# Row order, gate placement and the FFN boundary of a two-layer diffusion backbone kernel, changed together

## The chip, the cores and the metric

The kernel runs on one core of one Trainium2 chip. The metric is the device time of one execution in microseconds (us), lower is better. All times below come from runs of the kernel before or from one profiled execution of it. Engine names are those of the profile: PE is the matrix engine, PEld its weight loads, DVE the vector engine, ACT the scalar engine, POOL and SP two further engines that here mostly issue transfers.

## The reference, cut to what matters

Two token streams of 256 tokens each, latent `x` and context `ctx`, of width 1024, pass two layers. A layer is a half-step SwiGLU FFN, a token mixer, and a second half-step FFN; each has its own adaLN shift, scale and gate, which come from `silu(c)` and `silu(c_ctx)` times a 1024 x 9216 matrix `w_ada` per layer.

```
mod = (silu(c) @ w_ada[l] + b_ada[l]).reshape(9, 1024)
u = rmsnorm(h, g) * (1 + scale) + shift
h = h + 0.5 * gate * ((silu(u @ w1) * (u @ w3)) @ w2)          # w1, w3: 1024 x 2816
z = u @ w_in                                                   # q, kv, pool, linear attention, gates
m = sum_i sigmoid(gates_i) * (branch_i @ w_branch[i])          # attention, pooling, linear attention
h = h + gate * (m @ w_out)
```

The context stream takes part up to the mixer of the last layer, where it gives keys, values and the start states of the linear attention; the second FFN of the last layer works on the 256 latent tokens alone. Inputs, weights and the output are fp32.

## The kernel before, in words

**Products.** Activations lie feature-major: a tile has 128 features on its partitions and 512 tokens along it, latent tokens in columns 0 to 255, context tokens in 256 to 511. Every fp32 operand is split into a rounded part (`whi`, `uhi`, `hi`) and a remainder (`wlo`, `ulo`, `lo`), and a product is three matmuls (`mm3`, L238, L239, L240). The rounded part of a weight tile is made on ACT (L190) and the remainder on DVE (L202), from a tile `raw` that SP loads. `Weights.run_ahead` does this ahead of the products: at most four `raw` tiles are loaded, and parts are cut while no more than `room` of the tiles are held (`ROOM_FFN`, `ROOM_MIX`, 20 each; `ROOM_1`, `ROOM_2` in the first FFN). All these tiles come out of one pool of 70 slots.

**Order.** The program is written as generators that are advanced by credits. Every engine then runs its instructions in the order in which they were placed, and waits at each for what it needs. In the mixers the chain of attention and linear attention yields names of steps, and `FILL` gives for each step how many pieces of other work (`fill`: the columns of `w_in` for pools, linear attention and gates, then the branch projections) are put behind it. `GATES` is the number of gate pieces among those put in while the pooling branch is made. When no such work is left before the attention's outputs `oa` are complete, the filler yields without work.

**Modulation (`ada`).** The 36 pieces (layer, j) of 512 columns of `w_ada` are made in the order of need. The first four of layer 0 are loaded by SP and multiplied on PE (L370, then four transposes, L384), j in the order 0, 2, 1, 3. Nearly all others are multiplied on DVE (`adaacc`, L401 and L403; 16 per piece, on tiles that POOL's queue loads), behind other work. Two pieces, (0, 17) and (1, 17), stand in `EDGE`: their products are on PE, at the start of the second FFN of layer 0 and of layer 1.

**Start.** `setup` transposes the normalised rows `xr` of `x` and `ctx` (32 transposes, L324), makes `csil` by Silu on ACT, and transposes the raw rows into the residual `h` in two parts. The first FFN's first units of weights are split into halves of four k tiles each.

**FFN start.** `ffn` takes the mean square of the residual by a matmul (`ms`, L508), `rstd` on ACT, and then u tile by tile: `ut` on DVE (L517), `uhi` on ACT, `ulo` on DVE (L521). The last FFN ends in token-major form: `ht`, 16 transposes of the residual (L715), and the gate `gt` by a matmul with a diagonal `dg` (L728) stand behind the first four of its 22 up units.

Of the kernel before, what the change touches and what calls it, by code (L numbers as in the profile page):

```python
# [38 lines left out]
NHALF, NSLOT, ROOM_FFN, ROOM_MIX, RAWS = 4, 70, 20, 20, 4  # L39
RAWS_ADA = 3  # L40
ROOM_1, ROOM_2, LAST = 16, 36, 4
# [4 lines left out]
GATES = (2, 12)  # L46
EDGE = {(1, 17): (1, 2), (0, 17): (0, 2)}
# [93 lines left out]

class Net:
    def __init__(self, nc, a, cst, msk, vecs, wa2, out, pools, w, wada):
# [6 lines left out]
        self.ahead = self.seconds = None  # L150
# [83 lines left out]
    def mm3(self, out, wts, x, start, stop):  # L234

        (wh, wl), (xh, xl) = wts, x
        mm = self.nc.tensor.matmul
        mm(out, wh, xh, start=start, stop=False)  # L238
        mm(out, wh, xl, start=False, stop=False)  # L239
        mm(out, wl, xh, start=False, stop=stop)  # L240
# [12 lines left out]
    def setup(self):  # L253
# [39 lines left out]
        self.act(out=self.csil[:, :, 0:2], in_=self.vec[0][:, V_C:V_C + 16].rearrange("p (s k) -> p k s", s=2), func=AF.Silu)  # L293
# [5 lines left out]
        for j in range(4):  # L299
# [5 lines left out]
            self.act(out=f, in_=f, func=AF.Exp, scale=-0.5)  # L305
# [5 lines left out]
        self.residual(range(4), [normed])  # L311
        self.hr = []
        for k in range(KD):
            t = self.slot(name="hr")
            if k % 2:
                self.act(out=t, in_=self.turned(xr, k), func=AF.Copy)
            else:
                nc.vector.tensor_copy(t, self.turned(xr, k))
            self.hr.append(t)

    def turned(self, x, k):
        ps = self.ps()
        for j in range(4):
            self.nc.tensor.transpose(ps[:, j * P:(j + 1) * P], x[j][k // 4][:, (k % 4) * P:(k % 4 + 1) * P], self.ident)  # L324
        return ps

    def residual(self, ks, others=()):
        for k in ks:
            if k < 4:
                i = self.nc.vector.tensor_copy(self.h[:, k, :], self.turned(self.xin, k))  # L330
                if self.tc:
                    self.behind(i, others)
            else:
                self.act(out=self.h[:, k, :], in_=self.turned(self.xin, k), func=AF.Copy)
# [24 lines left out]
    def ada(self, l, j):  # L359
# [4 lines left out]
        if early or self.on_pe:  # L364
            ps = self.ps("ada")
            for u in range(4):
                for k in range(2 * u, 2 * u + 2):
                    unit = None if early else self.ada_unit(l, j, k)
                    g = k % 4
                    nc.tensor.matmul(ps[32 * g:32 * g + 32, :], self.csil[:, k, :], self.early[j][k] if early else unit.hi,  # L370
                                     start=(k < 4), stop=(k >= 4))
# [8 lines left out]
            if not early or j in (1, 3):  # L380
                yield
# [7 lines left out]
            if early:  # L389
                yield  # L390
                if j in (0, 2):
                    yield
# [106 lines left out]
    def norm(self, l, i, n):  # L499
# [11 lines left out]
        def some(s, c, ks):  # L511
            for k in ks:
                assert {(l, i, k // 4), (l, i + 1, k // 4)} <= self.have
                if u[k] is None:
                    u[k] = self.slot(F32R, "uhi"), self.slot(F32R, "ulo")
# [30 lines left out]
    def first_norm(self):  # L546
# [3 lines left out]
        for ks in ([0], [1], [2, 3], range(4, KD)):  # L550
            for k in ks:
# [3 lines left out]
                for s in range(2):  # L555
                    c = slice(s * NL, (s + 1) * NL)
                    t, a, b = self.half("ut"), self.am[0][1][:, k, s:s + 1], self.mod[0][:, k, s:s + 1]
                    self.act(out=hi[:, c], in_=self.hr[k][:, c], func=AF.Identity, scale=a, bias=b)
# [49 lines left out]
    def ffn(self, l, which, n, final):  # L608
# [10 lines left out]
        if begin:  # L619
            norm = self.first_norm()  # L620
            self.adas(5)
            self.residual(range(4, KD))
            self.xin = None
            self.adas(5)
# [14 lines left out]
            first[1].extend(part(1, [0]))  # L639

            def rest():
# [3 lines left out]
                first[1].extend(part(1, [1, 2]))  # L645

        else:
            self.w.room = ROOM_FFN
            first = unit(0) + unit(1)
# [12 lines left out]
        def up(m0, m1):  # L662
            for m in range(m0, m1):
                if m == 0:
                    if begin:
                        steps = [lambda: None, lambda: self.adas(4), lambda: self.adas(1), lambda: self.adas(4), rest]
# [40 lines left out]
        up(0, 4)  # L707
        assert {(l, 8, 0), (l, 8, 1)} <= self.have

        ht = []  # L710
        for j in range(2):
            for c in range(2):
                ps = self.ps()
                for k in range(4):
                    nc.tensor.transpose(ps[:, k * P:(k + 1) * P], self.h[:, 4 * c + k, j * P:(j + 1) * P], self.ident)  # L715
# [798 lines left out]
```

## Time and profile before

The median of three runs is 2119.14 us (2117.68 to 2120.08). The profiled execution took 2120.19 us; the profile spans 2118.4 us of it, so 1.8 us lie around the span.

| | value |
|---|---|
| PE busy | 2071.1 us (98% of the span) |
| DVE busy | 1449.1 us (68%) |
| ACT busy | 883.3 us (42%) |
| DMA | 290.48 MB, mean 137 GB/s |
| matmuls of `ps<-uhi,whi` and its two partners | 3 x 1584 |
| DVE `wlo` / ACT `whi` | 912 each |
| DVE `adaacc` L403 | 420, mean 746 ns |

Starts of matmuls that follow one another without a wait are closer together than the busy time of one (the engine overlaps them), so how long a group of products takes is read from the distance of starts. "Idle before" names what ended an idle stretch. The granted clock (PEclk) is the share of full speed that the matrix engine was given in a stretch.

By places: the first FFN of layer 0 runs to about 404 us (the mean squares `ms` that begin the stages mark the places), its mixer to 866, its second FFN to 1243, the first FFN of layer 1 to 1609, its mixer to 1906, and the last FFN to the end.

### The profile page before, as it was taken

Reading aid. Unit: us, or ns where it says so; the run is one execution under the profiler, and the core shown is the slowest. Engines: PE = TensorE matmul, PEld = TensorE weight load, DVE = VectorE, ACT = ScalarE, POOL = GpSimd, SP = SyncE. Lnnn points to the kernel's source line nnn. Section 1 sums busy time; section 2 is a strip of 40 time slices with the busy share of each in tenths; the row PEclk is TensorE's granted clock in tenths of the full one; section 3 lists DMA queues with packets and bytes.
Section 4 is the critical chain, followed back from the end, with each engine's and each line's share of the span. In section 5 each row is a group of like instructions: output and inputs, shape, how many; then the busy total and the mean of one; then the engine's idle time right before and its main releaser. Section 6 shows DMA issues by size and latency. Waiting matters only on the chain.

```text
span 2118.4 us, 30235 instructions
## 1 busy us (share of the span) xinstructions
PE 2071.1 (98%) x11308; PEld 1738.7 (82%) x11308; DVE 1449.1 (68%) x2876; ACT 883.3 (42%) x1805; POOL 138.4 (7%) x264
## 2 busy tenths in 40 slices
PE   7999999999999999999999999999999999998999
PEld 4888888977777888788888898888888887897997
DVE  4789588875877664766965886685554688665564
ACT  5423223464445553432322343322343566654452
POOL 0011011000100000101110100010000000000000
PEclk9999999999999999999999999999999999999999
DMA  9557456424423223445744645473451343565663
GB/s 319 150 157 206 125 170 169 118 59 122 137 75 83 67 70 95 130 139 139 216 132 131 173 125 154 110 224 114 121 151 36 102 119 85 140 169 145 182 205 121
DMA packets 416836, 290.48 MB, mean 137 GB/s; under 512 B 18608, under 2 KB 388912, under 8 KB 416688
## 3 DMA queue, kind: packets, MB, share of 16 engines
q1 hardware_dynamic: 395920, 221.22, 37.0%
q0 software_dynamic: 20480, 67.13, 11.1%
q8 instruction: 89, 1.46, 0.3%
q14 instruction: 59, 0.48, 0.1%
q10 hardware_dynamic: 288, 0.20, 0.0%
HBM read 287.44 MB, written 1.05 MB: 136 GB/s over the span
## 4 chain that ended last, share of the span: by engine, by line
PE 52%; issue 41%; DMA 3%; DVE 2%; POOL 1%; ACT 0%; SPq 0%; POOLq 0%; DVEq 0%; ACTq 0%
PE ps L238 14%; PE ps L240 14%; PE ps L239 14%; DMA raw<-in_w_ada_dram 2%; PE fill L238 2%; PE fill L240 2%; PE fill L239 2%; DMA ada<-in_w_ada_dram 1%; POOL raw L355 1%; PE sc L1145 1%; DVE adaacc L403 1%; PE ada L370 1%; PE pt L1163 0%; PE av L1181 0%; DVE wlo L202 0%
## 5 line engine op out<-in xcount | busy, mean ns | idle before, releaser
L202 DVE TENSOR_TENSOR wlo<-raw,whi 128x512 fp32r<-128x512 f32 (+4 forms) x912 | 532.5, 618 | 103.3 <-ACT whi L190 92.0
L238 PE MATMUL ps<-uhi,whi 128*128 128x512 f32 (+1 forms) x1584 | 555.4, 353 | 7.8 <-ACT uhi L190 7.8
L239 PE MATMUL ps<-ulo,whi 128*128 128x512 f32 (+1 forms) x1584 | 554.8, 351 | 0.2 <-DVE ulo L560 0.2
L240 PE MATMUL ps<-uhi,wlo 128*128 128x512 f32 (+1 forms) x1584 | 554.5, 351 | 0.0
L190 ACT ACTIVATE whi<-raw 128x512 fp32r<-128x512 f32 (+4 forms) x912 | 467.7, 567 | 173.6 <-DMA raw<-in_ffn_w_dram 53.7
L238 PEld LDWEIGHTS ps<-uhi,whi 128*128 128x128 f32 x1584 | 299.6, 190 | 54.1 <-ACT uhi L190 12.0
L240 PEld LDWEIGHTS ps<-uhi,wlo 128*128 128x128 f32 x1584 | 300.7, 190 | 46.1 <-issue 5.8
L239 PEld LDWEIGHTS ps<-ulo,whi 128*128 128x128 f32 x1584 | 300.9, 190 | 40.6 <-issue 1.9
L403 DVE SCALAR_TENSOR_TENSOR adaacc<-raw,csil,adaacc 128x512 f32<-128x512 f32 x420 | 303.9, 746 | 32.7 <-DMA raw<-in_w_ada_dram 32.1
L238 PE MATMUL ps<-hi,whi 128*128 128x512 f32 (+1 forms) x738 | 271.2, 368 | 1.5 <-ACT hi L190 1.5
L240 PE MATMUL ps<-hi,wlo 128*128 128x512 f32 (+1 forms) x738 | 269.9, 366 | 0.0
L239 PE MATMUL ps<-lo,whi 128*128 128x512 f32 (+1 forms) x738 | 269.6, 366 | 0.0
L190 ACT ACTIVATE silu<-ps 128x512 f32<-128x512 f32 (+1 forms) x88 | 47.8, 543 | 495.7 <-PE ps L240 495.7
L355 POOL DMA_DIRECT2D raw<-in_w_ada_dram x256 | 137.4, 537 | 1783.2 <-DVE adaacc L401 713.7
L659 DVE TENSOR_TENSOR silu<-silu,ps 128x512 f32<-128x512 f32 (+1 forms) x88 | 54.5, 619 | 245.7 <-PE ps L240 140.0
L238 PE MATMUL fill<-uhi,whi 128*128 128x512 f32 (+1 forms) x576 | 204.2, 355 | 3.9 <-ACT whi L190 3.9
L240 PE MATMUL fill<-uhi,wlo 128*128 128x512 f32 (+1 forms) x576 | 196.7, 342 | 0.2 <-DVE wlo L202 0.2
L239 PE MATMUL fill<-ulo,whi 128*128 128x512 f32 (+1 forms) x576 | 196.2, 341 | 0.0
L238 PEld LDWEIGHTS ps<-hi,whi 128*128 128x128 f32 x738 | 139.1, 189 | 24.0 <-ACT hi L190 1.7
L239 PEld LDWEIGHTS ps<-lo,whi 128*128 128x128 f32 x738 | 139.2, 189 | 22.6 <-DVE lo L202 0.2
L240 PEld LDWEIGHTS ps<-hi,wlo 128*128 128x128 f32 x738 | 139.2, 189 | 22.6
L238 PEld LDWEIGHTS fill<-uhi,whi 128*128 128x128 f32 x576 | 110.0, 191 | 26.2 <-issue 8.5
(279 smaller groups left out, 2304.8 us busy)
## 6 DMA issues: line engine op xcount, KB each, us to landing
raw<-in_ffn_w_dram SPq DMA_DIRECT2D x192, 512.0 KB, 4.7
raw<-in_w_ada_dram POOLq DMA_DIRECT2D x256, 256.0 KB, 3.4
raw<-in_w_in_dram SPq DMA_DIRECT2D x86, 512.0 KB, 4.5
raw<-in_ffn_w_dram SPq DMA_DIRECT2D x48, 384.0 KB, 4.4
raw<-in_ffn_w_dram SPq DMA_DIRECT2D x48, 320.0 KB, 3.8
raw<-in_w_branch_dram SPq DMA_DIRECT2D x48, 256.0 KB, 2.9
ada<-in_w_ada_dram SPq DMA_DIRECT2D x32, 256.0 KB, 5.4
raw<-in_w_out_dram SPq DMA_DIRECT2D x16, 512.0 KB, 5.0
```

Of the source, the lines that this page charges most:

```text
L190: i = self.nc.scalar.activation(**k)
L202: second = lambda: self.nc.vector.tensor_tensor(out=lo, in0=src, in1=f32hi, op=ALU.subtract)
L238: mm(out, wh, xh, start=start, stop=False)
L239: mm(out, wh, xl, start=False, stop=False)
L240: mm(out, wl, xh, start=False, stop=stop)
L355: self.nc.gpsimd.dma_start(out=t, in_=src)
L370: nc.tensor.matmul(ps[32 * g:32 * g + 32, :], self.csil[:, k, :], self.early[j][k] if early else unit.hi, start=(k < 4), stop=(k >= 4))
L403: nc.vector.scalar_tensor_tensor(out=acc[s], in0=unit.hi, scalar=c, in1=acc[s], op0=ALU.mult, op1=ALU.add)
L659: nc.vector.tensor_tensor(out=s[:, 0:n], in0=s[:, 0:n], in1=p3[:, 0:n], op=ALU.mult)
L1145: nc.tensor.matmul(sc[:, 0:nk], q[h][:, tt * P:(tt + 1) * P], keys[h][:, k0:T], start=True, stop=True)
```

## The change

**Constants.** `ROOM_MIX` becomes 20 for the first mixer and 28 for the second; `ROOM_1` goes from 16 to 12; `GATES` from (2, 12) to (4, 12); a new `LATER` (0, 16); `EDGE` is empty, so (0, 17) and (1, 17) are made on DVE as all the others.

**Start.** `csil` is made from Exp, an add, a reciprocal and a multiplication. Of the raw rows' 32 transposes 24 come first, then the products of j 0, then the transposes of `xr`, then the last 8. The first product of j 1 and of j 3 is placed behind the last weight product before it. The second halves of all three first units are cut one step earlier (`more`).

**Second mixer.** u lies in a tile for each stream (`ul`, `uc`: rounded part and remainder of the 256 tokens side by side), and the context's tiles are let go once the linear attention's columns are made. The columns for its keys are made as 2 x 256 instead of 512 tokens. While the attention's outputs are incomplete, gates 0 to 7 and 16 to 23 are put in rather than nothing.

**Last FFN.** `ht` is made before the mean square (`by_tokens`), and `gt` behind eight up units.

```diff
...
-NHALF, NSLOT, ROOM_FFN, ROOM_MIX, RAWS = 4, 70, 20, 20, 4
+NHALF, NSLOT, ROOM_FFN, ROOM_MIX, RAWS = 4, 70, 20, (20, 28), 4
 RAWS_ADA = 3
-ROOM_1, ROOM_2, LAST = 16, 36, 4
+ROOM_1, ROOM_2, LAST = 12, 36, 4
...
-GATES = (2, 12)
-EDGE = {(1, 17): (1, 2), (0, 17): (0, 2)}
+GATES = (4, 12)
+LATER = (0, 16)
+EDGE = {}
...
+class Streams:
+
+
+    def __init__(self, lat, ctx):
+        self.lat, self.ctx = lat, ctx
+
+    def __getitem__(self, at):
+        c = at[1]
+        assert c.stop <= NL or c.start >= NL
+        return self.lat[:, c] if c.stop <= NL else self.ctx[:, c.start - NL:c.stop - NL]
...
-        self.act(out=self.csil[:, :, 0:2], in_=self.vec[0][:, V_C:V_C + 16].rearrange("p (s k) -> p k s", s=2), func=AF.Silu)
+        c, e = self.vec[0][:, V_C:V_C + 16], self.tiny(16, "esil")
+        self.act(out=e, in_=c, func=AF.Exp, scale=-1.0)
+        nc.vector.tensor_scalar(out=e, in0=e, scalar1=1.0, scalar2=None, op0=ALU.add)
+        nc.vector.reciprocal(out=e, in_=e)
+        by_k = lambda t: t.rearrange("p (s k) -> p k s", s=2)
+        nc.vector.tensor_tensor(out=self.csil[:, :, 0:2], in0=by_k(c), in1=by_k(e), op=ALU.mult)
...
         self.xin = xin
-        self.residual(range(4), [normed])
+        self.residual(range(6), (normed, last))
+        self.adas(4)
         self.hr = []
         for k in range(KD):
             t = self.slot(name="hr")
             if k % 2:
-                self.act(out=t, in_=self.turned(xr, k), func=AF.Copy)
+                self.act(out=t, in_=self.turned(xr, k, self.products), func=AF.Copy)
             else:
-                nc.vector.tensor_copy(t, self.turned(xr, k))
+                nc.vector.tensor_copy(t, self.turned(xr, k, self.products))
             self.hr.append(t)
-
-    def turned(self, x, k):
+        self.residual(range(6, KD))
+        self.xin = None
+        self.adas(1)
...
+    def residual(self, ks, others=None):
         for k in ks:
-            if k < 4:
-                i = self.nc.vector.tensor_copy(self.h[:, k, :], self.turned(self.xin, k))
-                if self.tc:
-                    self.behind(i, others)
+            ps = self.turned(self.xin, k)
+            if k % 2:
+                i = self.act(out=self.h[:, k, :], in_=ps, func=AF.Copy)
             else:
-                self.act(out=self.h[:, k, :], in_=self.turned(self.xin, k), func=AF.Copy)
+                i = self.nc.vector.tensor_copy(self.h[:, k, :], ps)
+            if self.tc and others:
+                self.behind(i, [others[k % 2]])
...
+                    g = k % 4
                     unit = None if early else self.ada_unit(l, j, k)
-                    g = k % 4
-                    nc.tensor.matmul(ps[32 * g:32 * g + 32, :], self.csil[:, k, :], self.early[j][k] if early else unit.hi,
-                                     start=(k < 4), stop=(k >= 4))
+                    others = [self.last_product] if j in (1, 3) and not k else [self.products] if k else []
+                    self.products = nc.tensor.matmul(ps[32 * g:32 * g + 32, :], self.csil[:, k, :], self.early[j][k] if early else unit.hi,
+                                                     start=(k < 4), stop=(k >= 4))
+                    if early and self.tc:
+
+                        self.behind(self.products, others)
...
             ev = self.slot(name="adaev")
             self.evac = self.act(out=ev, in_=ps, func=AF.Copy)
-            if not early or j in (1, 3):
-                yield
+            yield
...
-                if j in (0, 2):
-                    yield
...
                 if u[k] is None:
-                    u[k] = self.slot(F32R, "uhi"), self.slot(F32R, "ulo")
+                    if (l, i) == (DEPTH - 1, 3):
+                        a, b = self.slot(F32R, "ul"), self.slot(F32R, "uc")
+                        u[k] = tuple(Streams(a[:, x:x + NL], b[:, x:x + NL]) for x in (0, NL))
+                    else:
+                        u[k] = self.slot(F32R, "uhi"), self.slot(F32R, "ulo")
...
             self.adas(5)
-            self.residual(range(4, KD))
-            self.xin = None
-            self.adas(5)
...
-            first[1].extend(part(1, [0]))
+
+            def more():
+                self.adas(1)
+                self.w.room = 2 * ROOM_1
+                first[1].extend(part(1, [0, 1, 2]))
 
             def rest():
                 self.adas(1)
                 next(norm)
                 self.w.room = ROOM_2
-                first[1].extend(part(1, [1, 2]))
+                self.w.run_ahead()
 
         else:
             self.w.room = ROOM_FFN
+            ht = self.by_tokens() if final else None
...
-                        steps = [lambda: None, lambda: self.adas(4), lambda: self.adas(1), lambda: self.adas(4), rest]
+                        steps = [lambda: None, lambda: self.adas(4), more, lambda: self.adas(4), rest]
...
-        up(0, 4)
+        up(0, 8)
+
         assert {(l, 8, 0), (l, 8, 1)} <= self.have
-
-        ht = []
-        for j in range(2):
...
-                ps = self.ps()
-                for k in range(4):
-                    nc.tensor.transpose(ps[:, k * P:(k + 1) * P], self.h[:, 4 * c + k, j * P:(j + 1) * P], self.ident)
-                t = self.slot(name="ht")
-                self.act(out=t, in_=ps, func=AF.Copy)
-                ht.append(t)
...
-        up(4, KF)
+        up(8, KF)
...
+    def by_tokens(self):
+
+        nc = self.nc
+        ht = []
+        for j in range(2):
+            for c in range(2):
+                ps = self.ps()
+                for k in range(4):
+                    nc.tensor.transpose(ps[:, k * P:(k + 1) * P], self.h[:, 4 * c + k, j * P:(j + 1) * P], self.ident)
+                t = self.slot(name="ht")
+                self.act(out=t, in_=ps, func=AF.Copy)
+                ht.append(t)
+        return ht
...
-        self.w.room = ROOM_MIX
+        self.w.room = ROOM_MIX[l]
...
-            for k in range(KD):
-                self.mm3(o[:, 0:m], unit.block(k), (u[k][0][:, 0:m], u[k][1][:, 0:m]), k == 0, k == KD - 1)
-                if k == 3:
-                    yield 1
+            streams = [slice(0, m)] if self.full or m == NL else [slice(0, NL), slice(NL, T)]
+            for c in streams:
+                for k in range(KD):
+                    self.mm3(o[:, c], unit.block(k), (u[k][0][:, c], u[k][1][:, c]), k == 0, k == KD - 1)
+                    if k == 3 and c is streams[0]:
+                        yield 1
...
             yield from glas()
+            for k in range(KD):
+                u[k] = tuple(t.lat for t in u[k])
         yield from pools()
...
+        later = [gate(j) for j in (*range(8), *range(16, 24))][0:LATER[l]]
         while len(self.oa) < 4:
-            yield 1
+            if later:
+                yield from later.pop(0)
+            else:
+                yield 1
         oa = [self.parts(t[:, 0:n], n) for t in self.oa]
         self.oa.clear()
         yield from branch(0, oa)
         oa.clear()
-        for dc in range(4):
-            yield from gate(16 + dc)
+        for dc in range(4 if self.full else 8):
+            if 16 + dc not in self.gates:
+                yield from gate(16 + dc)
...
```

**ACT in the start.** The first halves of the first three units are followed by the part for j 1, j 3 (`adaev`, the evacuation of their products) and the second halves (`whi`). Before:

```order
L190 ACTIVATE whi<-raw 128x512 x2
L190 ACTIVATE uhi<-hr,mod_170,am_1_172 128x256 x6
L190 ACTIVATE whi<-raw 128x512 x4
L190 ACTIVATE adaev<-ada 128x512 x2
L190 ACTIVATE uhi<-hr,mod_170,am_1_172 128x256 x8
```

Now:

```order
L203 ACTIVATE uhi<-hr,mod_170,am_1_172 128x256 x6
L203 ACTIVATE whi<-raw 128x512 x2
L203 ACTIVATE adaev<-ada 128x512
L203 ACTIVATE whi<-raw 128x512 x6
L203 ACTIVATE adaev<-ada 128x512
L203 ACTIVATE uhi<-hr,mod_170,am_1_172 128x256 x8
```

Two `whi` now stand ahead of j 1's `adaev` where four stood, and six stand between it and j 3's, where none stood.

**PE at the start of the last FFN.** `hilo` is the merged branch output, the last product of the mixer's output projection stands at the top. Before:

```order
L240 MATMUL ps<-hilo,wlo 128x256
L508 MATMUL ms<-acc,cst_72 128x256
L370 MATMUL ada<-raw,csil 32x512 x3
L238 MATMUL ps<-uhi,whi 128x256 x4
L239 MATMUL ps<-ulo,whi 128x256
L240 MATMUL ps<-uhi,wlo 128x256
L239 MATMUL ps<-ulo,whi 128x256
L240 MATMUL ps<-uhi,wlo 128x256
L239 MATMUL ps<-ulo,whi 128x256
L370 MATMUL ada<-raw,csil 32x512
```

Now:

```order
L253 MATMUL ps<-hilo,wlo 128x256
L786 MATMUL ps<-cst_72,h 128x128 x16
L534 MATMUL ms<-acc,cst_72 128x256
L251 MATMUL ps<-uhi,whi 128x256 x3
L252 MATMUL ps<-ulo,whi 128x256
L253 MATMUL ps<-uhi,wlo 128x256
L252 MATMUL ps<-ulo,whi 128x256
L253 MATMUL ps<-uhi,wlo 128x256
```

The products with `csil` (L370) are gone, and 16 transposes of the residual stand ahead of the mean square.

**PE in the attention of the second mixer.** `fill` are products for gates, `av`, `A`, `sc`, `ds`, `pt` and `o` steps of the two attentions. Before:

```order
L239 MATMUL fill<-ulo,whi 128x256
L240 MATMUL fill<-uhi,wlo 128x256
L1181 MATMUL av<-pT,v 64x256 x8
L1326 MATMUL A<-qt,kt 128x128 x8
L1145 MATMUL sc<-k,q 128x512 x2
L1344 MATMUL ds<-gv,ket 64x128 x28
L1163 MATMUL pt<-cst_72,p 128x128 x8
L1363 MATMUL o<-gv,Asum 128x128 x2
```

Now (each of the pieces of `fill` goes on for 12 rows on either side):

```order
L252 MATMUL fill<-ul,whi 128x256
L253 MATMUL fill<-ul,wlo 128x256
L1372 MATMUL A<-qt,kt 128x128 x8
L251 MATMUL fill<-ul,whi 128x256
L252 MATMUL fill<-ul,whi 128x256
L253 MATMUL fill<-ul,wlo 128x256
```

Where the steps stood back to back, `A` now has 12 products of a gate on either side.

More of the change, by code (lines that the diff above doesn't have):

```diff
@@ L149, in __init__ @@
         self.have = set()
-        self.ahead = self.seconds = None
+        self.ahead = self.seconds = self.products = None
         self.after, self.owed, self.on_pe, self.edge = iter(()), 0, False, []
@@ L239, in mm3 @@
         mm(out, wh, xl, start=False, stop=False)
-        mm(out, wl, xh, start=False, stop=stop)
+        self.last_product = mm(out, wl, xh, start=False, stop=stop)
     def parts(self, src, n=T):
@@ L304, in setup @@
             self.act(out=f, in_=f, func=AF.Ln, scale=1.0 / D, bias=self.eps[:, 0:1])
-            self.act(out=f, in_=f, func=AF.Exp, scale=-0.5)
+            last = self.act(out=f, in_=f, func=AF.Exp, scale=-0.5)
             xr.append([self.slot(name="xr") for _ in range(2)])
@@ L315, in setup, with turned @@
             if k % 2:
-                self.act(out=t, in_=self.turned(xr, k), func=AF.Copy)
+                self.act(out=t, in_=self.turned(xr, k, self.products), func=AF.Copy)
             else:
-                nc.vector.tensor_copy(t, self.turned(xr, k))
+                nc.vector.tensor_copy(t, self.turned(xr, k, self.products))
             self.hr.append(t)
-    def turned(self, x, k):
+        self.residual(range(6, KD))
+        self.xin = None
+        self.adas(1)
+    def turned(self, x, k, other=None):
         ps = self.ps()
         for j in range(4):
-            self.nc.tensor.transpose(ps[:, j * P:(j + 1) * P], x[j][k // 4][:, (k % 4) * P:(k % 4 + 1) * P], self.ident)
+            i = self.nc.tensor.transpose(ps[:, j * P:(j + 1) * P], x[j][k // 4][:, (k % 4) * P:(k % 4 + 1) * P], self.ident)
+            if other and self.tc:
+                self.behind(i, [other])
         return ps
-    def residual(self, ks, others=()):
+    def residual(self, ks, others=None):
         for k in ks:
-            if k < 4:
-                i = self.nc.vector.tensor_copy(self.h[:, k, :], self.turned(self.xin, k))
-                if self.tc:
-                    self.behind(i, others)
-            else:
-                self.act(out=self.h[:, k, :], in_=self.turned(self.xin, k), func=AF.Copy)
+            ps = self.turned(self.xin, k)
+            if k % 2:
+                i = self.act(out=self.h[:, k, :], in_=ps, func=AF.Copy)
+            else:
+                i = self.nc.vector.tensor_copy(self.h[:, k, :], ps)
+            if self.tc and others:
+                self.behind(i, [others[k % 2]])
     def setup_rest(self):
@@ L557, in first_norm @@
                     t, a, b = self.half("ut"), self.am[0][1][:, k, s:s + 1], self.mod[0][:, k, s:s + 1]
-                    self.act(out=hi[:, c], in_=self.hr[k][:, c], func=AF.Identity, scale=a, bias=b)
+                    self.users.append(self.act(out=hi[:, c], in_=self.hr[k][:, c], func=AF.Identity, scale=a, bias=b))
                     nc.vector.tensor_scalar(out=t, in0=self.hr[k][:, c], scalar1=a, scalar2=b, op0=ALU.mult, op1=ALU.add)
@@ L706, in ffn @@
             return
-        up(0, 4)
+        up(0, 8)
         assert {(l, 8, 0), (l, 8, 1)} <= self.have
-        ht = []
-        for j in range(2):
-            for c in range(2):
-                ps = self.ps()
-                for k in range(4):
-                    nc.tensor.transpose(ps[:, k * P:(k + 1) * P], self.h[:, 4 * c + k, j * P:(j + 1) * P], self.ident)
-                t = self.slot(name="ht")
-                self.act(out=t, in_=ps, func=AF.Copy)
-                ht.append(t)
         gt = []
```

## The prediction, made before the change was run

> **What bounds the kernel now.** I read the page first, then PE's waits over the whole span, then windows and timelines around the longest of them.
>
> ```profile
> span 2118.4 us, 30235 instructions
> ...
> PE 2071.1 (98%) x11308; PEld 1738.7 (82%) x11308; DVE 1449.1 (68%) x2876; ACT 883.3 (42%) x1805; POOL 138.4 (7%) x264
> ```
>
> Of the waits each row has the engine, the waiting matmul and what released it, then us in total, how often, and the longest.
>
> ```profile
> PE ps L238 <- ACT uhi L190: 7.8, 6, 1.8
> ...
> PE ada L370 <- DMA raw<-in_w_ada_dram: 4.1, 2, 3.2
> PE fill L238 <- ACT whi L190: 3.9, 1, 3.9
> PE ms L508 <- DVE acc L492: 3.7, 1, 3.7
> PE rq L1131 <- ACT rq L190: 3.2, 1, 3.2
> ...
> PE ot L1383 <- DVE mx L1149: 1.7, 1, 1.7
> ...
> PE o L1367 <- DVE st L1352: 1.2, 1, 1.2
> ...
> PE ps L728 <- DVE dg L727: 0.6, 1, 0.6
> ...
> PE ket L1305 <- DVE pT L1168: 0.5, 1, 0.5
> PE av L1181 <- ACT p L190: 0.4, 1, 0.4
> PE ket L1305 <- ACT pT L190: 0.4, 1, 0.4
> ```
>
> PE is busy for 98% of the span, so a shorter ACT or DVE stage gives nothing by itself. Time can come from three sources only: the 2118.4 - 2071.1 = 47.3 us in which PE idles, matmuls that leave PE, and stretches in which PE is busy but slow. For the last I asked windows around the waits. The first four rows have the stretch, its length, PE busy and its records, PEclk, DMA share and GB/s, the others PE, PEld, DVE, ACT and POOL ahead of PEclk; rows three and four give the pace without waits.
>
> ```profile
> 871.10:887.30 16.20, 12.97 (x55) 0.79 0.35 112
> 1913.50:1926.30 12.80, 11.74 (x48) 0.73 0.41 123
> ...
> 1820.00:1840.00 20.00, 20.00 (x169) 1.00 0.86 223
> 100.00:120.00 20.00, 20.00 (x90) 1.00 0.47 132
> ...
> 494.00:497.00 3.00, 2.98 (x9) 2.58 (x10) 1.46 (x4) 2.97 (x5) 0.00 (x0) 0.50 0.51 127
> 1701.00:1705.00 4.00, 3.62 (x16) 3.42 (x17) 4.00 (x10) 3.49 (x10) 0.00 (x0) 0.61 0.06 16
> 1760.00:1780.00 20.00, 19.09 (x143) 16.80 (x142) 18.07 (x37) 15.62 (x31) 0.00 (x0) 1.00 0.22 60
> 1780.00:1800.00 20.00, 18.40 (x181) 12.44 (x179) 16.69 (x47) 9.43 (x25) 0.00 (x0) 1.00 0.18 53
> ```
>
> A product of 256 tokens takes 20/169 = 0.118 us, one of 512 takes 20/90 = 0.222. Behind idle stretches of 3.2 us and more the granted clock falls to about a half for some 3 us, so such a wait costs its idle time and about 1.5 us more (3 us x 0.5 at 494; 4 us x 0.39 = 1.6 at 1701).
>
> **The change part by part.** Terms go against the profiled execution, 2120.2 us; it lies 1.1 above the median of the runs, 2119.1.
>
> *Second FFN of layer 0: EDGE empty.*
>
> ```profile
> 869.66 1.06 PE L370 MATMUL ada<-raw,csil 128*32 128x512 f32 x6
> 871.16 0.74 PE L238 MATMUL ps<-uhi,whi 128*128 128x256 f32 x4 [0.44 <-ACT uhi L190]
> ...
> 876.70 1.91 PE L370 MATMUL ada<-raw,csil 128*32 128x512 f32 x2 [3.17 <-DMA raw<-in_w_ada_dram]
> ```
>
> Of the 55 records in 871.1 to 887.3, 10 belong to the `ada` products (the other 6 of 16 stand before, in a gap that ends with `uhi` anyway and gives nothing) and 2 to `ms`; 43 products remain, 43 x 0.118 + 0.5 for `ms` = 5.6 us of 16.2. The rest, 10.6, is transfer wait, half clock and the `ada` products themselves, and goes. With the four transposes later about 10.8. The feed of u does not take the place of the wait: one k tile costs DVE `ut` and `ulo` (about 0.48 each by the row below) and PE twelve products (1.4 us). Low bound 7, should DVE's feed fall behind after all; high 11.2. The 2 x 16 instructions on DVE cost, with the row's 746 ns, 2 x 16 x 0.75 = 24 us, a few more with the reductions, spread over stretches where DVE has 30% free by the page; without that cover they would stand ahead of `wlo`, at their own 24 us.
>
> ```profile
> L403 DVE SCALAR_TENSOR_TENSOR adaacc<-raw,csil,adaacc 128x512 f32<-128x512 f32 x420 | 303.9, 746 | 32.7 <-DMA raw<-in_w_ada_dram 32.1
> ...
> L521 DVE SCALAR_TENSOR_TENSOR ulo<-ut,mod,uhi 128x256 fp32r<-128x256 f32 x72 | 33.1, 477 | 8.5 <-ACT uhi L190 8.2
> ```
>
> *Last FFN.* The same accounting: 12.8 us hold 48 records, 10 of them `ada`; 38 x 0.118 = 4.5, so 8.3 us go.
>
> ```profile
> 1909.80 0.96 PE L508 MATMUL ms<-acc,cst 128*128 128x256 f32 x2 [3.74 <-DVE acc L492]
> 1910.69 1.93 PE L370 MATMUL ada<-raw,csil 128*32 128x512 f32 x6
> 1913.59 1.22 PE L238 MATMUL ps<-uhi,whi 128*128 128x256 f32 x4 [0.97 <-ACT uhi L190]
> ...
> 1945.70 1.91 PE L715 MATMUL ps<-cst,h 128*128 128x128 f32 x16
> ```
>
> The 16 transposes (1.9 us) move from 1945 into the 3.74 us gap ahead of `ms`, the `dg` wait (0.6) is covered by four more up units, four `ada` transposes go (0.4). Against this, four `ht` copies and a `whi` stand ahead of or between the two `rstd` on ACT: u some 0.8 us later. The transposes break the idle stretch before `ms`, but with the `ada` products gone PE idles from `ms` to the first u, more than 3 us, and the half clock may stay: half of 1.5 is 0.8. Sum 8.3 + 1.9 + 0.6 + 0.4 - 0.8 - 0.8 = 9.6; bounds 7 and 12.
>
> *First mixer: GATES 4.* 36 products of 512 tokens, 8.0 us, move ahead of `rq`, 24 of them into its wait. The chain to `rq` is on ACT and DVE, and their queues change by three splits. Gain 3.2 + 1.5 = 4.7; bounds 3 and 5.5.
>
> *Second mixer: room 28.*
>
> ```profile
> 1696.21 1.29 ACT L190 ACTIVATE e<-e 128x512 f32<-128x512 f32 x2
> 1699.65 0.63 ACT L190 ACTIVATE e<-b 128x512 f32<-128x512 f32 x1 [2.15 <-DVE b L1289]
> 1700.18 0.40 ACT L190 ACTIVATE hilo<-pooled 128x256 fp32r<-128x256 f32 x1
> 1700.49 0.61 ACT L190 ACTIVATE whi<-raw 128x512 fp32r<-128x512 f32 x1
> ```
>
> The `whi` that PE waits 3.9 us for stands behind an `e` that waits for DVE. With more room this part is cut before the first `e`. The price of the wait is 3.9 + 1.6 = 5.5; the next unit's part takes its place in ACT's queue, though, and may make PE wait a little: I take 4.5, bounds 0 (the wait moves one unit on) and 5.5.
>
> *Second mixer: LATER 16.* Between 1777 and 1804 PE runs the steps of both attentions with no gate between, and waits 0.4 + 0.5 + 0.4 + 1.2 + 1.7 = 4.2 us, from the rows above. Twelve gates, 24 x 12 x 0.118 = 34 us, now stand there instead of behind. The waits go: 4.2; bounds 0 and 8 (small gaps between short matmuls that a gate's products might close). The work is moved, not removed. DVE has 18.07 and 16.69 of 20 us there and gets 24 `wlo` at 0.69 (34 us longer window, 16.6 us more work), so it stays below PE.
>
> *Second mixer: streams.* Two key tiles of 24 products at 512 tokens become 2 x 24 at 256: 48 x (2 x 0.118 - 0.222) = 0.7 us lost.
>
> *Start.*
>
> ```profile
> 42.29 0.63 ACT L190 ACTIVATE whi<-raw 128x512 fp32r<-128x512 f32 x1 [0.20 <-DMA raw<-in_ffn_w_dram]
> ...
> 43.46 0.66 PE L384 MATMUL ada<-cst,adaev 128*128 128x128 f32 x4 [1.06 <-ACT adaev L190]
> ...
> 50.18 0.60 PE L384 MATMUL ada<-cst,adaev 128*128 128x128 f32 x4
> ...
> 41.52 4.48 SPq L229 DMA_DIRECT2D raw<-in_ffn_w_dram  x4
> ...
> raw<-in_ffn_w_dram SPq DMA_DIRECT2D x4, 256.0 KB, 4.5
> ```
>
> The earlier products and one wait less (1.06 us) would bring PE to j 3's transposes some 2.5 us before 50.18, with the same 54 products done. But six `whi` now stand ahead of j 3's `adaev` on ACT, and the last needs the last of four transfers that SP issues up to 46.00. With 4.5 us to land (3.6 at the least, as an estimate from the shorter of such transfers) that is about 49.6, and with the 43.46 - 42.29 = 1.17 us from such a `whi` to the transposes 50.8. So the gain ends there: +0.6, and the idle time of about 3 us may bring the half clock; I take +1.0, bounds -2 and +4. The Trainium skill, page "TensorE: Matmul & The Clock Gate", section "HAM oscillation — how this bites in real kernels", says that gaps of more than about 3.4 us throttle the matrix engine; the waits of 3.2 to 3.9 us here agree, and it speaks against this part. By that rule alone, and with an idle stretch over its limit, the start would be 0.6 + 1.5 = 2.1 us slower, not 1.0.
>
> Sum: -10.8 - 9.6 - 4.7 - 4.5 - 4.2 + 0.7 + 1.0 = -32.1 us. 2120.2 - 32.1 = 2088.1, and against the median 2087.
>
> **The rivals.**
>
> *The second mixer gives nothing.* Room and LATER move waits instead of removing them: the next late `whi` follows the first, and DVE, 90% busy at 1760 to 1780, becomes the bound where gates add `wlo`. For it: that 18.07. Against: 34 us more of PE time come with the 16.6 us of DVE work. Time: 2087 + 8.7 = 2096.
>
> *Half clock where it was broken.* Start, `ms` to u in the last FFN, and the second FFN of layer 0 each pay 1.5 more: 2087 + 4.5 = 2091.5. For it: every idle stretch over 3.2 us in the windows was followed by it. Against: a `uhi` wait of 1.8 us is the longest of its kind, and the transposes break the gap.
>
> *Slower: gates starve between the attention's steps.* A gate's weights take a transfer (4.5 us), `whi` (0.62) and `wlo` (0.69) before its first product. If slots or `raw` tiles come free only when the gate before is done, each of the twelve costs 5.8 us in place of 2.8, and the attention's steps in PE's queue wait behind it: 12 x 3.0 = 36 us, 2087 + 36 = 2123. It decides from the point where the second mixer holds all 70 slots. Against: transfers moved only 53 to 60 GB/s there, of 223 at 1820; and the context's half of u is free by then.
>
> *The change hides less than it says.* If EDGE's pieces on DVE come late, `uhi` of the FFN waits for them: 2087 + 10 = 2097.
>
> **How the numbers follow.** Forecast as summed, 2080 to 2093: 0.60. Second mixer nothing: 0.14. Half clock: 0.10. EDGE late: 0.06. Starved gates: 0.05, and something of that size that I do not see, 0.01 slower and 0.04 within 0.2%. A difference below 0.2%, some 4 us, is one that a measurement here cannot tell from no change. Faster 0.90, within 0.2% 0.04, slower 0.06. The gains' low bounds together (7 + 7 + 3 + 0 + 0 - 0.7 - 4 = 12) give 2107, the high ones (11.2 + 12 + 5.5 + 5.5 + 8 - 0.7 + 2 = 43.5) 2076; neither set comes as a whole. I take 2074 to 2104, the lower end 2 us further for what the new order may close elsewhere; the likeliest case's own range stands above.
>
> **What would show it.** No L370 after 100 us and PEclk 1.00 where 871 to 887 and 1913 to 1926 stand; no `rq` wait in the first mixer; no `fill <- whi` wait in the second; no waits of `o`, `ot`, `av`, `ket`; a wait of `ada` for `adaev` near 50 us of about 3 us. I am wrong if PE's idle time does not fall from 47 us to about 30, or if DVE `wlo` or `adaacc` releases PE in several places.

## The result and the profile after

The change takes 2095.75 us (median of four runs, 2094.67 to 2096.01) where the kernel before takes 2118.74 (2117.68 to 2120.08): the ratio is 0.989, 95% interval 0.9873 to 0.9907. It is faster by 23 us. I had forecast 2087, so 32 us; the time lies inside the range of 2074 to 2104, but outside the 2080 to 2093 that I had given 0.60. The two profiled executions differ by a little more than the medians: their spans are 2118.4 and 2092.9, so 25.5 us. The execution profiled before took 2120.19, 1.4 over its median, the one after 2094.67, 1.1 under its own; these 2.5 us are the spread of runs, not the change.

The page of the change, its first two parts:

```profile
span 2092.9 us, 30290 instructions
...
PE 2056.7 (98%) x11320; PEld 1739.6 (83%) x11320; DVE 1475.0 (70%) x2923; ACT 880.0 (42%) x1802; POOL 138.9 (7%) x264
```

PE's idle time fell from 47.3 to 2092.9 - 2056.7 = 36.2 us, not to the 30 that I had named, and DVE took 26 us more, most of it for the two pieces of `EDGE` (with them back on PE, in the first experiment below, DVE is busy for 1450.9 us). PE's waits in the change (waiting matmul and what released it, us in total, times, the longest) say which waits are gone and which are new:

```profile
PE ps L251 <- ACT uhi L203: 10.1, 5, 3.8
...
PE pool L251 <- ACT hilo L203: 4.0, 3, 1.8
PE ada L412 <- ACT adaev L203: 3.0, 2, 2.2
PE ps L751 <- DVE dg L750: 1.9, 1, 1.9
...
PE ket L1351 <- ACT pT L203: 0.5, 1, 0.5
PE ket L1351 <- DVE pT L1214: 0.4, 1, 0.4
PE sc L1191 <- DVE scal L1179: 0.4, 1, 0.4
```

The waits for the `ada` tiles, `rq`, the late `whi`, `st` and `mx` are gone. New are `pool` for `hilo` (4.0 us in three), a `uhi` of 3.8 us, the `adaev` of 2.2 us, and the `dg` wait grew from 0.6 to 1.9. The two waits of `ket` (0.5 and 0.4), which the prediction had gone, stay.

Where the time went shows best by stages in the two traces, the first from the start of the span, the others from the start of a stage's last pair of `ms` matmuls, each to the first `ms` of the next stage (the 5.6 to 6.8 us between the `ms` of one stage are in no row, and are as long in both). The second mixer ends at its last product, and the last row runs from there to the last matmul:

| stage | before | change | difference | forecast |
|---|---|---|---|---|
| start and first FFN, layer 0 | 397.12 | 398.67 | +1.6 | +1.0 |
| mixer, layer 0 | 462.19 | 457.70 | -4.5 | -4.7 |
| second FFN, layer 0 | 370.99 | 359.93 | -11.1 | -10.8 |
| first FFN, layer 1 | 359.39 | 359.66 | +0.3 | 0 |
| mixer, layer 1 | 290.30 | 286.30 | -4.0 | -8.0 |
| last FFN, from that product on | 207.57 | 199.82 | -7.8 | -9.6 |

Four rows are right within 0.6 us in these two executions. The second mixer gave half of what was forecast, and the last FFN 1.8 us less. These two rows are what the experiments are about, beside the question whether the right rows are right for the reason given. Two rows vary from execution to execution: the first takes 396.96 to 399.55 us in the nine profiled executions with the change's start, the second mixer 285.4 to 288.0 in the eight with the change's mixer. Three windows of the change (stretch, length, PE busy and its records, PEclk, DMA share, GB/s) show two of the right rows at once, and a half clock that stayed:

```profile
868.81:884.31 15.50, 15.50 (x130) 1.00 0.00 1
1894.70:1906.00 11.30, 11.28 (x73) 0.74 0.16 46
...
478.00:498.00 20.00, 20.00 (x92) 1.00 0.29 83
```

The second FFN of layer 0 from its last `ms` on and the place of `rq` run at full pace without a gap: 130 records in 15.5 us are 0.119 us each. The start of the last FFN does not: 0.74 of the clock.

### The profile page after: what moved, and what is told of

It is laid out like the page before. It is cut to its first block, busy times and chain, and to the rows that moved or that the text cites. A ratio compares the mean times of both kernels' runs of the same rounds, so it can differ in the third digit from the quotient of the medians.

```text
span 2092.9 us, 30290 instructions
## 1 busy us (share of the span) xinstructions
PE 2056.7 (98%) x11320; PEld 1739.6 (83%) x11320; DVE 1475.0 (70%) x2923; ACT 880.0 (42%) x1802; POOL 138.9 (7%) x264
## 4 chain that ended last, share of the span: by engine, by line
PE 92%; ACT 3%; DMA 2%; DVE 2%; issue 1%; SPq 0%; ACTq 0%; DVEq 0%
PE ps L251 23%; PE ps L253 23%; PE ps L252 23%; PE fill L251 4%; PE fill L253 4%; PE fill L252 4%; PE sc L1191 1%; DMA ada<-in_w_ada_dram 1%; PE av L1227 1%; PE gv L251 1%; PE gv L253 1%; PE gv L252 1%; PE pt L1209 1%; ACT whi L203 1%; ACT L199 0%
## 5 line engine op out<-in xcount | busy, mean ns | idle before, releaser
L251 PE MATMUL ps<-uhi,whi 128*128 128x512 f32 (+1 forms) x1536 | 543.0, 355 | 10.1 <-ACT uhi L203 10.1
L252 PE MATMUL ps<-ulo,whi 128*128 128x512 f32 (+1 forms) x1536 | 542.4, 354 | 0.2 <-DVE ulo L590 0.2
L253 PE MATMUL ps<-uhi,wlo 128*128 128x512 f32 (+1 forms) x1536 | 541.5, 353 | 0.0
L429 DVE SCALAR_TENSOR_TENSOR adaacc<-raw,csil,adaacc 128x512 f32<-128x512 f32 x448 | 325.1, 747 | 37.4 <-DMA raw<-in_w_ada_dram 36.6
L253 PEld LDWEIGHTS ps<-uhi,wlo 128*128 128x128 f32 x1536 | 292.2, 190 | 40.0 <-DVE wlo L215 0.6
L252 PEld LDWEIGHTS ps<-ulo,whi 128*128 128x128 f32 x1536 | 292.7, 191 | 39.3 <-DVE ulo L590 0.6
L251 PE MATMUL fill<-uhi,whi 128*128 128x512 f32 x288 | 117.9, 409 | 0.0
L253 PE MATMUL fill<-uhi,wlo 128*128 128x512 f32 x288 | 112.8, 392 | 0.0
L252 PE MATMUL fill<-ulo,whi 128*128 128x512 f32 x288 | 112.3, 390 | 0.0
L251 PE MATMUL fill<-ul,whi 128*128 128x256 f32 x288 | 86.2, 299 | 0.0
```

Source lines behind the costliest of these rows:

```text
L253: self.last_product = mm(out, wl, xh, start=False, stop=stop)
L429: nc.vector.scalar_tensor_tensor(out=acc[s], in0=unit.hi, scalar=c, in1=acc[s], op0=ALU.mult, op1=ALU.add)
```

## The experiments

The kernels of one group ran on one chip together with the kernel before. Times of whole kernels are medians; times of stages and waits come from one profiled execution of each.

### Is each gain its own edit's?

**The two pieces of `EDGE` back on PE.**

```diff
-EDGE = {}
+EDGE = {(1, 17): (1, 2), (0, 17): (0, 2)}
```

> The change with the two EDGE pieces back on PE (nothing left out). If the wait for the ada tiles, their products and the half clock were the price, the second FFN of layer 0 is again 11 us longer (371 us between its last ms and the next FFN's first, not 360), and the last FFN some 5 us longer, since its ten late products and their 1.0 us wait come back while the half clock stands there already: 2096 + 16 = 2112. If the gain came from the moved transposes and gates instead, only 8 us come back: 2104.

2111.4 us (ratio to the kernel before 0.9964, 0.9951 to 0.9977), so 15.7 us of the 23 hang on this one line. The second FFN of layer 0 takes 369.87 us instead of 359.93, and the old picture is back, the transfer in front of the products (PE's timeline):

```profile
865.59 1.06 PE L396 MATMUL ada<-raw,csil 128*32 128x512 f32 x6
...
872.52 1.91 PE L396 MATMUL ada<-raw,csil 128*32 128x512 f32 x2 [3.06 <-DMA raw<-in_w_ada_dram]
```

The last FFN, from the mixer's last product on, is 5.0 us longer, as expected. The first FFN of layer 1 is 359.38 with the pieces on PE and 359.66 with them on DVE: DVE's share there for such pieces (`adaacc` and what follows from it) rises from 93.3 to 121.7 us, and costs 0.3.

**The same line alone in the kernel before.**

```diff
-EDGE = {(1, 17): (1, 2), (0, 17): (0, 2)}
+EDGE = {}
```

> The kernel before with EDGE empty and nothing else. The terms of the prediction for it alone: second FFN of layer 0 10.8 us shorter, last FFN up to 8.7 shorter: 2118.7 - 19 = 2100. In the last FFN the idle stretch from ms to the first u is then 3.8 us long and the half clock should stay behind it, so that some 2 us of this are lost: 2102. If the pieces on DVE come late, less: 2105 and more.

2103.0 us (0.9927, 0.9912 to 0.9942): 15.7 us less than the kernel before, the same as taken out of the change. The part does not lean on the others. As expected the half clock stays where the gap to the first u is left open, here the window of 1902 to 1906 (as above, with PEld, DVE, ACT and POOL ahead of PEclk):

```profile
1902.00:1906.00 4.00, 2.25 (x10) 2.25 (x11) 3.78 (x9) 3.59 (x7) 0.00 (x0) 0.50 0.82 210
```

**No gates between the steps of the attention.**

```diff
-LATER = (0, 16)
+LATER = (0, 0)
```

> The change with LATER (0, 0): no gates between the attention steps of the second mixer. If they hide the waits, o for st, ot for mx and av for p come back (4.2 us before) and small gaps with them: 2096 + 5 = 2101. If DVE is the bound there and the waits only moved, the time stays: 2096.

2100.5 us (0.9916, 0.9902 to 0.9931), 4.7 more than the change, and two of the waits of before are back (`av` for `p` is not, and `ket` had never gone):

```profile
PE ot L1429 <- DVE mx L1195: 1.8, 1, 1.8
...
PE o L1413 <- DVE st L1398: 0.9, 1, 0.9
```

From the second `logit` to the mixer's last product this kernel takes 143.4 us and the change 138.0. DVE is not the bound there. The forecast had 4.2 from five waits. The windows of that stretch, first without gates, then the change, show that idle time makes 3.2 of the 5.4 us, and that the same instructions keep PE busy for 2.2 us less:

```profile
1750.09:1893.48 143.39, 139.18 (x1135) 1.00 0.45 124
```

```profile
1750.01:1888.02 138.01, 136.99 (x1134) 1.00 0.47 129
```

**Two gates in place of four in the first mixer.**

```diff
-GATES = (4, 12)
+GATES = (2, 12)
```

> The change with GATES (2, 12). If the 36 products cover the wait for rq, that wait comes back with 3.2 us idle and about 1.5 us of half clock: 2096 + 4.5 = 2100.5. If other parts of the change shortened the chain to rq, less: 2097.

2098.0 us (0.9901, 0.9884 to 0.9917). The wait is back at its place with its old length, and the first mixer takes 462.15 us instead of 457.70:

```profile
494.19 1.11 PE L1177 MATMUL rq<-cst,rq 128*128 128x128 f32 x4 [3.18 <-ACT rq L203]
```

So the stage shows 4.45 us, as expected, and the medians 2.3, half of what was expected. The other stages of this execution are together 0.8 us shorter than in the profile of the change, the start alone 1.4; the last section says what varies there.

### Why did the larger room give nothing?

```diff
-NHALF, NSLOT, ROOM_FFN, ROOM_MIX, RAWS = 4, 70, 20, (20, 28), 4
+NHALF, NSLOT, ROOM_FFN, ROOM_MIX, RAWS = 4, 70, 20, (20, 20), 4
```

(The line also holds the constants that stay.)

> The change with room 20 in the second mixer. The prediction's account: the wait of fill for whi (3.9 us) and its half clock come back: 2096 + 4.5 = 2100.5. The rival, which the trace of the change suggests: the pooled branch's hilo stands behind the same e on ACT as the late whi did, so PE waits there with either room, and the time is the same within 1 us: 2095 to 2097.

2095.56 us (0.989, 0.9875 to 0.9905), the change's own 2095.75 within 0.2 us. The rival of the expectation holds. With room 20 PE waits for the late `whi`:

```profile
1689.02 0.39 PE L251 MATMUL fill<-ul,whi 128*128 128x256 f32 x1 [3.97 <-ACT whi L203]
```

With room 28 that part is cut in time, and PE reaches its next instruction, a product of the pooled branch. ACT's timeline of the change there, and the product:

```profile
1686.67 0.63 ACT L203 ACTIVATE e<-b 128x512 f32<-128x512 f32 x1 [2.15 <-DVE b L1335]
1687.20 0.40 ACT L203 ACTIVATE hilo<-pooled 128x256 fp32r<-128x256 f32 x1
...
1687.66 0.39 PE L251 MATMUL pool<-hilo,whi 128*128 128x256 f32 x1 [1.82 <-ACT hilo L203]
```

`hilo` stands in ACT's queue behind the same `e` as the `whi` did, and `e` waits for DVE's scan. So 2.1 us of the 4 are gained here, and given back at the next two products of `pool` (0.7 and 1.5), which do not wait with room 20: the chain of gated attention and pooling is late as a whole. In these two executions the same half clock stands behind both waits (below).

**The pooled branch's product one step later.**

```diff
-POOL = (1, 1)
+POOL = (1, 2)
```

> The change with the pooled branch's product one step of the chain later in the second mixer. If the waits of pool for hilo (4.0 us in three) are what ate the gain of the larger room, they go, since fill stands there instead: 2096 - 4 = 2092. If the chain is late as a whole, another instruction waits in their place: 2096.

2094.4 us (0.9887, 0.9873 to 0.9902), 1.3 less than the change, where 4 or nothing was expected. The `pool` waits are gone, a short one of `qsum` (0.9) comes, and one long wait stands in their place, further on:

```profile
PE sc L1191 <- DVE pT L1214: 3.8, 1, 3.8
```

In its trace the second `logit` stands 144.1 us after the mixer's `ms` instead of 148.8, and the last `av` at 228.7 instead of 228.0. What was saved in the first part was lost at this `sc`, by the wait and by the half clock behind it:

```profile
1759.50:1765.00 5.50, 5.50 (x20) 0.50 0.29 86
```

That is the second theory of the expectation, nearly.

### What the start and the last FFN still lose

**The start: one second half ahead of j 3's `adaev`, not three.**

```diff
-                self.w.room = 2 * ROOM_1
-                first[1].extend(part(1, [0, 1, 2]))
+                self.w.room = ROOM_1 + 4
+                first[1].extend(part(1, [0]))
...
                 self.w.room = ROOM_2
-                self.w.run_ahead()
+                first[1].extend(part(1, [1, 2]))
```

> The change with only the first of the three second halves cut ahead of j 3's adaev (room 16 there; the other two behind it, as before). If that adaev waits for the last raw, as the prediction says, the 2.2 us wait near 50 us goes, with the half clock behind it: first FFN 2 to 3 us shorter, 2096 - 2.5 = 2093. If the products behind need those halves at once, the wait moves there and the time stays: 2096.

2092.0 us (0.9876, 0.9862 to 0.9891), 3.7 less than the change. In the change the last of the six `whi` waits for its transfer, and `adaev` and PE behind it:

```profile
49.20 0.63 ACT L203 ACTIVATE whi<-raw 128x512 fp32r<-128x512 f32 x1 [0.24 <-DMA raw<-in_ffn_w_dram]
49.73 0.58 ACT L203 ACTIVATE adaev<-ada 128x512 f32<-128x512 f32 x1
...
50.37 1.07 PE L412 MATMUL ada<-cst,adaev 128*128 128x128 f32 x4 [2.21 <-ACT adaev L203]
```

With the edit PE reaches these transposes at 47.53 and does not wait:

```profile
47.53 0.60 PE L412 MATMUL ada<-cst,adaev 128*128 128x128 f32 x4
```

The first FFN takes 394.58 us, 2.5 less than before the change. So the new start does gain as a whole (its parts were not run alone), and six `whi` in the wrong place took it away.

**The last FFN: PE kept at work between `ms` and u.**

```diff
...
+                self.ahead = self.norm(l, i, n)
+                next(self.ahead)
+                warm = self.ps("warm")
+                for x in range(24):
+                    nc.tensor.transpose(warm[:, x % 4 * P:(x % 4 + 1) * P], self.h[:, x % KD, 0:P], self.ident)
```

> The change plus 24 transposes whose result nobody reads, between the mean square and the first u product of the last FFN (2.6 us of PE in a gap of 4.2 us). If the idle stretch there is what halves the clock, PEclk stays near 1.00 behind it instead of 0.50 from 1895 to 1899, and the last FFN is about 1.7 us shorter: 2094. If the clock falls for another reason, or the half clock is hidden by the feed of u, nothing changes: 2096.

2092.6 us (0.9879, 0.9864 to 0.9893), 3.1 less than the change; by the traces the stretch from the first u product to the end is 190.68 us instead of 193.11. The transposes do nothing but keep PE at work, and the first u comes no sooner (4.48 and 4.53 us behind `ms`). The window behind the gap, first in the change, then here:

```profile
1894.00:1898.00 4.00, 3.28 (x15) 0.50 0.45 131
```

```profile
1894.00:1898.00 4.00, 2.77 (x24) 1.00 0.40 111
```

24 records in 2.8 busy us against 15 in 3.3. The gap is what halves the clock.

**`dg` made earlier.**

```diff
-        up(0, 8)
+        up(0, 4)
+        dgs = []
+        for c in range(2):
+            dg = self.slot(name="dg")
...
+            dgs.append(dg)
+        up(4, 8)
...
-            nc.tensor.matmul(ps, ones[:, 0:P], dg, start=True, stop=True)
+            nc.tensor.matmul(ps, ones[:, 0:P], dgs[c], start=True, stop=True)
```

> The change with dg made on DVE four up units earlier than the matmul that needs it. The wait of 1.9 us for dg goes: 2096 - 1.9 = 2094. If dg's eight instructions delay a silu product on DVE where they now stand, the wait moves: 2096.

2092.4 us (0.9877, 0.9861 to 0.9894), 3.4 less than the change. The same stretch as above is 191.21 us, 1.9 less. Only 1.1 of this is the wait. The half clock at the start of the stretch lasts for 5.8 us of it in the profile of the change and for 3.4 here, which makes 1.2, and the rest of the stretch is 0.4 longer. What is left of the wait is for `ones`, which had stayed at its place:

```profile
PE ps L755 <- DVE ones L752: 0.8, 1, 0.8
```

**All three, and with the pooled product one step later.**

> The change with three edits at once: only one second half cut ahead of j 3's adaev, 24 transposes without a reader between ms and the first u product of the last FFN, and dg with its ones made four up units earlier. If the three waits are independent, the gains add: 2.5 in the first FFN, 2.4 and 1.9 + 0.8 in the last by the profiles of the single runs, 2095.5 - 7.6 = 2088. If one of them is taken up by the next wait, 2090 to 2092.

> The same with the pooled branch's product one chain step later. The chain in the second mixer sets the pace there by the account of the room: no difference beyond 1 us to the kernel without it, 2088. If the 3.8 us wait of sc in the single run was an accident of that order, 2085.

The edits are those above; in both, `ones` moves with `dg`. 2088.2 us (0.9857, 0.9841 to 0.9873) and 2085.7 us (0.9846, 0.9831 to 0.9860). The three gains add as the traces of the single runs had it (7.6 expected, 7.5 found); the differences of the single medians, 3.7, 3.1 and 3.4, would have given 10.2. In the first of these two traces the stretch from the first u product to the end is 188.52 us. No half clock stands there, nor in the kernel with the transposes alone (190.68), so the difference of 2.2 is the price of `dg` and `ones` free of the clock. The fourth edit gives 2.5 more, where the account of the late chain had none: the mixer is 284.83 us against 287.75. Its long wait is the one of the single run, so that wait is no accident of that order, and the time is gained all the same:

```profile
PE sc L1202 <- DVE pT L1225: 3.8, 1, 3.8
```

The account of the late chain is therefore only part of it. Without the `pool` waits the stretch near 1690, at half clock in the change, runs at full clock in the single run:

```profile
1690.00:1692.00 2.00, 2.00 (x19) 1.00 0.11 33
```

But most of the 2.9 us between the two mixers is the clock. PE's idle time there differs by 0.6. Without the fourth edit two stretches of 3.41 us run at half clock, from 1684.5 and from 1725.5, and with it one, from 1756.0, behind `sc`; 3.41 us at half cost 1.7. Windows inside them, first without the edit:

```profile
1684.60:1687.60 3.00, 3.00 (x16) 0.50 0.03 5
1725.60:1728.60 3.00, 3.00 (x16) 0.50 0.61 151
```

```profile
1756.00:1759.00 3.00, 3.00 (x9) 0.50 0.49 147
```

The mixer without the edit has none to two such stretches, depending on the execution (none in the kernel with `dg` earlier, 285.4 us). How much of the 2.5 us belongs to the edit is therefore open. 2085.7 us is the fastest kernel of this study, 10 us under the change and 33 under the kernel before.

**The change once more, beside these two.**

> The change itself beside these, on the same chip: 2095.75 as before, for the differences to it.

2095.9 us (0.9891, 0.9876 to 0.9905), with runs from 2091.8 to 2098.0. The 1.3 to 3.7 us of the single edits lie within this spread, so what each of them does is read from its waits and stages, and not from the medians alone.

## Why the prediction was right in its direction and 9 us short of its size

**`EDGE` and the first mixer** were right in place and size: 10.8 forecast and 11.1 found, 4.7 forecast and 4.5 found. Both times the sum was the idle time of one wait and the half clock behind it, for `EDGE` with the matmuls that leave; undoing the line alone brings both back in the stage (by the medians of the whole kernel, the first mixer's only in half).

**LATER** came out near its size, 4.2 forecast and 4.7 found, but not by its sum. Of the five waits the two of `ket`, 0.9 us, stay with gates between the steps; the other three, 3.4 us before, go. What made up for it is 2.2 us less busy time for the same instructions. The sum had put that at nothing and named it only in a bound, as small gaps between short matmuls; whether it is that was not separated. So the nearness of the two numbers is in part luck. The rival by which DVE becomes the bound falls; so does the slower one, of gates that starve, since the gates' products stand there without a wait for their weights.

**The start** was right in its mechanism: `adaev` behind six `whi`, of which the last waits for its transfer. I had PE at 50.8, it came at 50.37, and the half clock followed (the windows of the change), +1.6 against +1.0:

```profile
50.00:52.00 2.00, 1.64 (x6) 0.61 1.13 299
52.00:54.00 2.00, 2.00 (x6) 0.53 1.11 280
```

That the size fits is in part luck. In this execution a second half clock, near 30 us, adds to it, which the sum did not have (last section). Of the nine profiled executions with this start, five have half the clock near 50 us, and a first FFN of 398.67 to 399.55 us. Four have the wait (1.5 to 2.8 us) with the full clock behind it, and 396.96 to 397.57 us, where the old start took 397.12 and 397.69. One of these four, the kernel without gates in the attention:

```profile
50.00:52.00 2.00, 1.74 (x10) 1.00 1.14 303
```

**Room 28 was wrong.** The step was "I take 4.5, bounds 0 (the wait moves one unit on) and 5.5". It was the lower bound, 0. The reason stood in the rows that the step quoted: between the `e` and the `whi` there stood `hilo<-pooled`, held by the same `e`, and the products of `pool` follow in PE's order. I followed the `whi` to its user and did not ask who waits for the instruction one row above. With 0.7 for the split key tiles and 5.3 gained at the gates (from the second `logit` to the mixer's last product, 143.3 and 138.0 us), and 0.6 lost on the way, the whole stage is 4.0 shorter instead of 8.0.

**The last FFN** gave 7.8 instead of 9.6. Of its terms "the `dg` wait (0.6) is covered by four more up units" failed: the wait is 1.9. More work on PE ahead of `dg` covers nothing, since DVE has `dg`'s eight instructions in its queue behind the silu product of the last of those units; PE and DVE get there together. Half of a half clock, my 0.8, was the whole one: the gap from `ms` to the first u is 4.5 us, and with it filled 2.4 us are gained.

By the table the profiles fall 6.6 us short of the sum: 4.0 in the second mixer, 1.8 in the last FFN, 0.8 in the other rows. The other 2.2 of the 9 us lie between the profiled executions and the medians. The sign of being wrong that I had named shows the same: PE's idle time is 6 us above the 30, and 5.9 us are the new waits of `pool` (4.0) and `dg` (1.9).

The rival "the second mixer gives nothing" named 2096 and its number fits, but it is half true: room gave nothing, LATER gave the size of its term. That the time fits is a coincidence with the `dg` wait and the spread. The rival of late `EDGE` pieces named 2097, as near, and is false: the second FFN of layer 0 gained what was forecast. The rival of the half clock was right at two of its three places, the start (not in every execution) and the last FFN.

The Trainium skill, page "TensorE: Matmul & The Clock Gate", section "HAM oscillation — how this bites in real kernels", which the prediction weighed at the start, holds for the last FFN too: a 4.5 us gap with 3.8 us of waiting, half clock behind it, and none once 24 transposes stand in the gap.

## What to carry to other kernels

When a late instruction is moved ahead of what holds it, look at its neighbours in the same queue: whatever else stands behind the holder is now the one that is waited for. Work placed ahead of a wait covers it only if the awaited instruction does not itself stand behind that work, here a product of the same units on DVE. And a gap of some microseconds on PE can be filled with matmuls that nobody reads, if they are done before the awaited product could start: here they cost nothing, and the clock stayed full.

## What was not expected of the hardware

The prediction took the half clock to need idle stretches of 3.2 us and more. It also follows shorter ones, and not in every execution. In the start PE waits 1.81 us for `uhi`, with the same length before (until 30.21) and in the change (until 28.85). Behind it the clock is full in the first and half in the second (windows as above, before first):

```profile
30.00:32.00 2.00, 1.61 (x6) 1.04 (x7) 2.00 (x6) 2.00 (x5) 0.00 (x0) 1.00 1.06 389
```

```profile
30.00:32.00 2.00, 2.00 (x6) 1.51 (x6) 2.00 (x7) 2.00 (x5) 0.00 (x0) 0.50 1.06 388
1690.00:1692.00 2.00, 2.00 (x11) 2.00 (x11) 2.00 (x6) 2.00 (x7) 0.00 (x0) 0.50 0.12 25
```

The last row is the stretch behind the 1.82 us wait of `pool`: half the clock, as behind the 3.97 us of the kernel with room 20, where the same stretch reads

```profile
1690.00:1692.00 2.00, 2.00 (x11) 0.50 0.00 0
```

So half the wait had the same half clock behind it. And it need not: in the kernel with `dg` earlier the same wait of `pool` (1.82 us, until 1687.99) has the full clock behind it:

```profile
1688.00:1690.00 2.00, 2.00 (x16) 1.00 0.03 8
1690.00:1692.00 2.00, 2.00 (x21) 1.00 0.06 11
```

The same code in the same order thus differs by about 1.5 us from one execution to the next at each such place, and the first FFN of kernels whose start is the same reads 396.96 to 399.55 us (without gates in the attention, and the change beside the last group).

The fourteen traces show what decides here. In each of them the changes of the granted clock lie whole multiples of 3.413 us apart (in the change half clock begins at 29.97, 50.45, 1688.85 and 1893.65), so that time falls into steps of this length. From 20 to 2075 us, 46 steps at full clock have 1.82 us or more of idle PE, and half clock follows every one; with 1.50 to 1.81 us it follows 8 of 35, and with less none. So the 1.82 us wait of `pool` halves the clock when it lies inside one step, and not when a border between two steps cuts it, as the border at 1686.71 does in the kernel with `dg` earlier. That is a count over these traces; no run was made to test it.

The Trainium skill, page "TensorE: Matmul & The Clock Gate", section "What's actually happening", says that the window which decides is free-running, so that the transition point varies between runs; the run-to-run difference agrees. Its figure of at least one idle window of about 3.4 us does not fit the two waits of 1.8 us, nor, strictly, those of 3.2 us that the prediction counted as agreeing, and here the measurement decides.
